# A hybrid gMLP / RG-LRU / HGRN2 layer on one core: empty steps in the heads, set-ups in pieces, earlier loads, another order of the column groups

## Chip, cores and metric

The kernel runs on one core of one Trainium2 chip. The metric is the device time of one execution in microseconds (us). TensorE (PE in the rows) does the matrix products, VectorE (DVE), ScalarE (ACT) and GpSimd (POOL) the elementwise work, SyncE (SP) issues most of the loads. POOL also issues DMAs: all spills, the loads that read a spill back, and the loads that add to what is in place. Each engine works through its own queue in order.

## What is computed

One layer for two groups of rows, 512 prompt rows and 32 sample rows, which share all weights (T = 544 rows, D = 2048):

```python
mod = silu(c) @ w_ada + b_ada
h = rmsnorm(x, norm_g) * (1 + scale) + shift
z = h @ w_in                      # 2048 x 15360
au, av, ag, lx, lg, hq, hf, hi, hg, mg = split(z)
ya = gmlp_mix(gelu(au), rmsnorm(gelu(av)), ws, bs) * silu(ag)
yb = rglru(causal_conv(lx)) * silu(lg)
yc = rmsnorm(hgrn2(silu(hq), hf, hi)) * silu(hg)      # 8 heads, chunks of 64 rows
out = (sigmoid(ga) * (ya @ wb0) + sigmoid(gb) * (yb @ wb1) + sigmoid(gc) * (yc @ wb2)) @ w_out
y = rmsnorm(x + gate * out, final_g)
```

The new states of the three branches are outputs as well.

## The kernel before

Everything is transposed: channels lie on partitions, the 544 rows in the free dimension. Each weight block is split into a high part `wh` (ScalarE, L190) and a low part `wl` (VectorE, L232), and each product is made of three matmuls (`rows3`, L324): wh by the high part of x, wh by its low part, wl by the high part. The product z = h @ w_in (stage z) is made in 60 groups, each of two column blocks of 128; `Group` (from L337) forms the two blocks by seven products of half size in place of eight. So a group has seven **items**, each with 24 large matmuls (128x128 by 128x272), and stage z has 420 items. The second product of a pair needs sums of weight halves: one half is loaded by SP (ring `raw`, five slots, or ring `q`, two slots), the other is added to it in place by a DMA that POOL issues (L266).

The main loop (from L1404) goes over the items. For item i it issues loads (`feed`), then the additions that are due (`load_adds`), then splits the weights of items up to i + 2 (`AHEAD`), then the products of item i and their eviction, and at last calls `pump()`. `load_some` looks nine items ahead, `load_q` six, and both stop where the ring has no free slot; the addition to a q block is put five items ahead of its use.

`pump()` advances every background generator by one step, to its next `yield`: these are the small jobs that use the columns as they come. One step per item is thus their clock. The generators are `av_gen` and `gm_gen` (gMLP), `hg_gen` (one HGRN2 head at a time, 29 items each), `lru_gen` (RG-LRU), `put_away` (a gate, then the spill of a block to DRAM, L1134) and `y_gen` (loads a branch's result, L1199, and splits it for the merges). They share an arena of 32 units in SBUF: a buffer that one has freed is soon taken by another, which then waits until the DMA that spills it has read it.

A head (`hg_gen`) loads `hf` and `hq` (L739), and after two steps makes the gates. Its chunk products go by levels: `lev_d` (POOL, L789) makes differences, `lev_e` exponents (ScalarE), `lev_w` multiplies by k and q (VectorE, L804), `lev_mm` makes the products on TensorE (L815, L817), and `lev_put` (L826) puts them into place. Later come `ew` (VectorE, L882), a one-column product (L885), the load of `hi` (L888), transposes and products (L900 to L972), the load of S0 (L937, on SP), `newton` (L226), the scaling of o (L988) and the transposes of the result (L1003). `hg_setup` (L708) and `lru_setup` (L1017) compute constants once, the first in head 0's first step, the second in the first RG-LRU `post`.

The order of the groups is written out in `z_groups`: four av groups, then sixteen times a head's group (hf with hq, or hi with hg) and a light one (mg, the merge gates, which are only spilled), four light ones, then the 16 heavy ones (gMLP, RG-LRU) with a light one behind every four. A head can start when the spill of its hg is issued.

## Time and profile before

| | us |
|---|---|
| median of 3 runs | 2205.09 (2199.73 to 2208.75) |
| profiled execution, its own time | 2206.34 |
| its span, first to last instruction | 2204.6 |
| mean granted clock of TensorE | 0.956 |

The page of the profile gives for each engine its busy time and its share of the span. A granted clock of 1.00 is TensorE's 2.4 GHz, 0.50 its lower level of 1.2 GHz. From about 133 us to 1671 us stage z runs: the av groups until 244, the heads until 1207, gMLP until 1408, RG-LRU until 1671. Then come the three merges and the output product. In a row of waits the engine that waited stands first, with the line of its waiting instruction, then what ended the wait.

### The profile page before, as it was taken

How to read it: one execution, taken by the hardware profiler on the slowest of the kernel's cores; microseconds unless marked ns; L12 is line 12 of the kernel's file. 1: busy time of each engine (PE TensorE's matmuls, PEld its weight loads, DVE VectorE, ACT ScalarE, POOL GpSimd, SP SyncE). 2: the span in 40 equal slices, each digit the busy share in tenths (PEclk: the TensorE clock that was granted, in tenths of full speed). 3: DMA queues.
4: the chain of work that ended last, by engine and by line, in shares of the span. 5: the costliest groups of instructions: out<-in, count | busy, mean ns of one | idle time of the engine just before them, and what ended most of it. 6: DMA issues, size and time to landing. Idle time of an engine off the chain costs nothing.

```text
span 2204.6 us, 40701 instructions
## 1 busy us (share of the span) xinstructions
PE 2041.6 (93%) x15864; PEld 1945.3 (88%) x15864; DVE 1282.3 (58%) x2204; ACT 1103.0 (50%) x2137; POOL 503.4 (23%) x720
## 2 busy tenths in 40 slices
PE   5789998989998989898999999999987999999997
PEld 3279988989898989897989999999887999999996
DVE  3365665665766575856575766678675433442226
ACT  3357544655555555554554656567565433332223
POOL 0002122232313141313133222112223222220112
PEclk8789998989999999998999999999999999999998
DMA  8977675756665666665667777666655667665554
GB/s 313 365 190 189 187 187 150 189 158 180 168 187 159 179 165 182 162 190 146 188 161 203 188 198 199 180 156 171 166 147 192 232 185 185 195 196 173 174 173 168
DMA packets 135009, 412.22 MB, mean 187 GB/s; under 512 B 16128, under 2 KB 38432, under 8 KB 134816
## 3 DMA queue, kind: packets, MB, share of 16 engines
q1 hardware_dynamic: 87408, 261.08, 35.3%
q0 software_dynamic: 41424, 138.34, 27.7%
q10 hardware_dynamic: 5984, 10.19, 1.5%
q8 instruction: 125, 2.05, 0.4%
q14 instruction: 68, 0.56, 0.1%
HBM read 363.77 MB, written 45.78 MB: 186 GB/s over the span
## 4 chain that ended last, share of the span: by engine, by line
PE 70%; DMA 8%; DVE 7%; issue 6%; ACT 6%; POOL 2%; DVEq 0%; SPq 0%; ACTq 0%; POOLq 0%
PE pm L324 41%; PE pp L324 21%; DMA q<-in_w_in_dram 3%; ACT arena L190 2%; DVE wl L232 2%; ACT wh L190 2%; PE px L815 1%; DMA d_mg<-arena 1%; PE px L1286 1%; PE px L498 1%; PE px L571 1%; DMA raw<-in_w_ss_dram 1%; DVE x L232 1%; POOL arena L789 1%; DMA arena<-d_hf 1%
## 5 line engine op out<-in xcount | busy, mean ns | idle before, releaser
L324 PE MATMUL pm<-x,wh 128*128 128x272 f32 x6720 | 1316.8, 295 | 49.2 <-ACT arena L190 22.6
L324 PEld LDWEIGHTS pm<-x,wh 128*128 128x128 f32 x6720 | 1088.8, 194 | 58.3 <-ACT arena L190 25.0
L324 PE MATMUL pm<-x,wl 128*128 128x272 f32 x3360 | 987.1, 294 | 2.4 <-DVE wl L232 2.4
L232 DVE TENSOR_TENSOR wl<-raw,wh 128x512 fp32r<-128x512 f32 x652 | 458.1, 729 | 385.0 <-ACT wh L190 381.4
L324 PEld LDWEIGHTS pm<-x,wl 128*128 128x128 f32 x3360 | 649.2, 193 | 4.4 <-DVE wl L232 4.2
L190 ACT ACTIVATE wh<-raw 128x512 fp32r<-128x512 f32 x652 | 391.4, 624 | 334.3 <-PE pm L324 238.3
L324 PE MATMUL pp<-x,wh 128*128 128x272 f32 x2560 | 487.6, 290 | 5.9 <-ACT x L190 2.6
L324 PEld LDWEIGHTS pp<-x,wh 128*128 128x128 f32 x2560 | 402.2, 189 | 20.5 <-issue 13.5
L232 DVE TENSOR_TENSOR wl<-q,wh 128x512 fp32r<-128x512 f32 x360 | 256.1, 737 | 225.9 <-ACT wh L190 224.6
L324 PE MATMUL pp<-x,wl 128*128 128x272 f32 x1280 | 369.4, 289 | 0.0
L190 ACT ACTIVATE wh<-q 128x512 fp32r<-128x512 f32 x360 | 215.5, 624 | 137.7 <-PE pm L324 98.7
L190 ACT ACTIVATE arena<-arena 128x544 f32<-128x544 f32 (+5 forms) x310 | 162.8, 554 | 209.5 <-DVE arena L1339 76.7
L324 PEld LDWEIGHTS pp<-x,wl 128*128 128x128 f32 x1280 | 241.4, 189 | 0.2 <-DVE wl L232 0.2
L190 ACT ACTIVATE arena<-pm 128x272 f32<-128x272 f32 x240 | 93.8, 391 | 182.8 <-PE pm L324 139.8
L266 POOL DMA_DIRECT2D q<-in_w_in_dram x60 | 53.5, 892 | 503.4 <-DMA q<-in_w_in_dram 184.0
L365 DVE TENSOR_TENSOR q<-q,raw 128x1024 f32<-128x1024 f32 x120 | 148.7, 1239 | 4.1
L190 ACT ACT_TABLE_LOAD x59 | 75.7, 1283 | 13.1 <-DVE arena L1063 5.3
L266 POOL DMA_DIRECT2D raw<-in_w_in_dram x60 | 54.1, 902 | 107.7 <-DMA raw<-in_w_in_dram 52.2
L789 POOL TENSOR_TENSOR arena<-arena 128x544 f32<-128x544 f32 (+1 forms) x40 | 52.6, 1327 | 60.1 <-PE px L817 18.3
L815 PE MATMUL px<-arena 128*128 128x128 f32 x160 | 32.4, 333 | 26.9 <-DVE arena L804 17.2
L1242 DVE TENSOR_TENSOR arena<-pp,arena 128x544 f32<-128x544 f32 x48 | 34.7, 723 | 37.0 <-PE pp L324 37.0
L1349 POOL TENSOR_TENSOR tail<-tail,arena 128x544 f32<-128x544 f32 (+1 forms) x15 | 18.6, 1242 | 149.5 <-ACT arena L190 149.5
(265 smaller groups left out, 1425.6 us busy)
## 6 DMA issues: line engine op xcount, KB each, us to landing
raw<-in_w_in_dram SPq DMA_DIRECT2D x240, 512.0 KB, 4.7
q<-in_w_in_dram SPq DMA_DIRECT2D x60, 512.0 KB, 5.0
q<-in_w_in_dram POOLq DMA_DIRECT2D x60, 512.0 KB, 6.3
raw<-in_w_in_dram POOLq DMA_DIRECT2D x60, 512.0 KB, 7.4
raw<-in_w_branch_dram SPq DMA_DIRECT2D x48, 512.0 KB, 4.1
raw<-in_w_ss_dram SPq DMA_DIRECT2D x44, 512.0 KB, 7.0
raw<-in_w_out_dram SPq DMA_DIRECT2D x38, 512.0 KB, 4.6
raw<-in_w_gate_dram SPq DMA_DIRECT2D x32, 512.0 KB, 4.6
```

What stands on the lines that cost most here:

```text
L190: return nc.scalar.activation(out, in_, func, **kw)
L232: tt(lo, src, hi.bitcast(F32), op=OP.subtract)
L266: nc.gpsimd.dma_start(out=raws[n], in_=src, accum_op=OP.add)
L324: mm(p, a, rhs(k, r), start=start and i == 0 and q == 0, stop=stop and i == n - 1 and q == 2, **kw)
L365: tt(raws[n], raws[n], raws[m], op=OP.add)
L498: mm(st["xss"][h][:, :HF], ones, st["sq"][q % 2][:, i, h * HF:(h + 1) * HF], start=q == 0 and i == 0, stop=q == 7 and i == 1)
L571: mm(p[32 * i:32 * i + 2, part * 256:part * 256 + 256], cs[:, 4 * q + i, :], w[:, i * 256:(i + 1) * 256], start=q == 0, stop=q == 3)
L789: ptt(v, fv(src, 0, [[2 * m, nb], [m - 1, 2], [1, m]]), fv(src, m - 1, [[2 * m, nb], [0, 2], [0, m]]), op=OP.subtract)
L815: mm(fv(p, 64 * i, [[128, 2], [1, 64]]), x[:, 256 * i + 128:256 * i + 256], fv(x, 256 * i, [[256 + m, 2], [2 * m, nb], [1, m]]), start=Tru ...
L1242: tt(two(g.ap), halves(p), two(g.ap), op=OP.mult)
L1286: mm(p[32 * i:32 * i + 2, :256], cs[:, 4 * q + i, :], w[:, i * 256:(i + 1) * 256], start=q == 0, stop=q == 3)
L1349: ptt(a[:, n], a[:, n], b.ap[:, n], op=OP.add)
```

## The change

It adds one `yield` in `hg_gen` between `lev_w` and `lev_mm` for levels 16 and 8, for 4 and 2, and for 1, and one behind `newton`; a head takes 32 items. `hg_setup` and `lru_setup` become generators of their own with a `yield` between their parts; they start with head 0's first group and with the last light group ahead of the heavy ones. The loads of hf and hq are a function of their own, which the head before calls near its end. `hi` is loaded one step earlier, S0 by POOL instead of SP. Every `put_away` starts with a `yield`. `load_q` looks ten items ahead. The order of the groups has both groups of head 0 first, then a light group in front of each head's group, eight light ones ahead of the heavy ones, and one behind every eight of these. gMLP's `gm_gen` starts with the group's item 6 instead of its item 1. `y_gen` waits three steps between load and use, but for the second half of y0, and splits the first half in twos.

```diff
@@ -716,21 +716,26 @@
         nc.gpsimd.memset(hg["A"].ap, 0.0)
         t = hbuf(len(LEVELS) * 256)
         nc.gpsimd.dma_start(out=t.ap, in_=consts[:, 130:130 + len(LEVELS) * 256])
+        for _ in range(3):
+            yield
         nc.vector.tensor_copy(masks.rearrange("p a e n -> p (a e n)"), t.ap)
         t.free()
+        yield
         d, lb, l1, ln1 = (lbt[:, i, :] for i in range(4))
         x = P("lb", 0, 8)
         tt(d, x, x, op=OP.subtract)
+        yield
         act(d, d, AF.Exp)
+        yield
         nc.vector.reciprocal(lb, d)
         tt(lb, lb, d, op=OP.mult)
         tt(lb, lb, lb, op=OP.subtract)
         ts(l1, lb, -1.0, 1.0, op0=OP.mult, op1=OP.add)
+        yield
         act(ln1, l1, AF.Ln)
-
-    def hg_gen(h):
-        if h == 0:
-            hg_setup()
+        hg["ready"] = True
+
+    def hg_load(h):
         zf = hbuf()
         kq = [hbuf(T), hbuf(T + 1)]
         kb, qb = sorted(kq, key=lambda b: b.col)
@@ -738,8 +743,18 @@
         for b, n in ((zf.ap, "hf"), (qb.ap[:, 1:], "hq")):
             nc.gpsimd.dma_start(out=b, in_=scratch[f"{n} {h}"])
         nc.gpsimd.memset(qb.ap[:, 0:1], 0.0)
-        yield
-        yield
+        hg["in", h] = zf, kb, qb
+
+    def hg_gen(h):
+        while "ready" not in hg:
+            yield
+        if ("in", h) not in hg:
+            hg_load(h)
+            yield
+            yield
+            yield
+        yield
+        zf, kb, qb = hg.pop(("in", h))
         lb, l1, ln1 = (lbt[:, i, h:h + 1] for i in range(1, 4))
         t1, t2, g = hbuf(), hbuf(), zf
         KO = qb.col - kb.col
@@ -839,6 +854,7 @@
         lev_w(16)
         lev_w(8)
         yield
+        yield
         p1, p2 = lev_mm(16), lev_mm(8)
         lev_d(4)
         lev_d(2)
@@ -850,6 +866,7 @@
         yield
         lev_w(4)
         lev_w(2)
+        yield
         yield
         p1, p2 = lev_mm(4), lev_mm(2)
         xs[1].free()
@@ -881,11 +898,12 @@
         ew = ew_t[:, h % 2]
         tt(ew[:, :4], fv(eq.ap, 64, [[128, 4]]), fv(eq.ap, 128, [[128, 4]]), op=OP.mult)
         nc.vector.tensor_copy(ew[:, 4:5], eq.ap[:, T:T + 1])
+        zi = hbuf()
+        nc.gpsimd.dma_start(out=zi.ap, in_=scratch[f"hi {h}"])
+        yield
         p1 = lev_mm(1)
         mm(p1[:NS, 272:273], ke.ap[:, NP:], qb.ap[:, T:T + 1], start=True, stop=True)
         xs[0].free()
-        zi = hbuf()
-        nc.gpsimd.dma_start(out=zi.ap, in_=scratch[f"hi {h}"])
         yield
         nc.vector.tensor_copy(A[:NS, AS + NS:AS + NS + 1], p1[:NS, 272:273])
         lev_put(1, p1)
@@ -934,7 +952,7 @@
         zi.free()
         ke.free()
         s0 = hbuf(256)
-        nc.sync.dma_start(out=s0.ap[:, :128], in_=S0[:, h, :])
+        nc.gpsimd.dma_start(out=s0.ap[:, :128], in_=S0[:, h, :])
         yield
         act(kt.ap, pk, AF.Copy)
         act(vk.ap[:NS], pq[:NS, :256], AF.Copy)
@@ -984,6 +1002,7 @@
         act(r, r, AF.Exp, scale=-0.5)
         yield
         newton(r, m, t)
+        yield
         osb = hbuf(256)
         tt(ob.ap[:, :NP].rearrange("p (w n) -> p w n", w=4), o[:, :NP].rearrange("p (w n) -> p w n", w=4),
            fv(r, 0, [[1, 4], [0, 128]]), op=OP.mult)
@@ -992,6 +1011,8 @@
         at.free()
         vk.free()
         qe.free()
+        if heads["ready"] > h + 1:
+            hg_load(h + 1)
         yield
         nc.gpsimd.dma_start(out=S_new[0, h], in_=S.ap[:, 384:])
         nc.gpsimd.dma_start(out=S_new[1, h], in_=s0.ap[:, 128:])
@@ -1021,7 +1042,9 @@
         e, u, u2, acc, c8, n8 = (lru_c[:, i, :] for i in range(6))
         ts(e, x, -1.0, None, op0=OP.mult)
         tt(e, e, x, op=OP.min)
+        yield
         act(e, e, AF.Exp)
+        yield
         ts(u2, e, 2.0, None, op0=OP.add)
         nc.vector.reciprocal(acc, u2)
         tt(u, e, acc, op=OP.mult)
@@ -1030,6 +1053,8 @@
         for n in (17, 15, 13, 11, 9, 7, 5, 3, 1):
             tt(acc, acc, u2, op=OP.mult)
             ts(acc, acc, 1.0 / n, None, op0=OP.add)
+            if n % 4 == 3:
+                yield
         tt(acc, acc, u, op=OP.mult)
         ts(e, x, -1.0, 0.0, op0=OP.mult, op1=OP.max)
         stt(acc, acc, 2.0, e, op0=OP.mult, op1=OP.add)
@@ -1044,8 +1069,6 @@
             nc.gpsimd.dma_start(out=w[0].ap, in_=lru_w[b].rearrange("p a n -> p (a n)"))
 
         def post(x, lg):
-            if b == 0:
-                lru_setup()
             start(lru_gen(b, x, lg, w[0]))
         return post, fetch
 
@@ -1121,8 +1144,8 @@
 
         def put_away(n, o, on=None):
 
+            yield
             if n[:2] in ("hq", "hg"):
-                yield
                 t = buf()
                 act(t.ap, o.ap, AF.Sigmoid)
                 yield
@@ -1141,10 +1164,7 @@
             def post(*os):
                 for n, o in zip(names, os):
                     g = put_away(n, o, on if n == names[-1] else None)
-                    if n[:2] in ("hq", "hg"):
-                        start(g)
-                    else:
-                        next(g)
+                    start(g)
             return post
 
         def on_head(h):
@@ -1166,14 +1186,16 @@
             heavy.append((B_AU + g, B_AG + g, post, lambda g=g, cell=cell: start(gm_gen(g, cell))))
         for b in range(8):
             heavy.append((B_LX + b, B_LG + b, *lru_post(b)))
-        todo = av
-        for i in range(16):
-            todo += [head[i], light[i]]
-        todo += light[16:20]
-        rest = iter(light[20:])
+        todo = av + head[:2]
+        todo[4] += ({1: lambda: start(hg_setup())},)
+        for i in range(14):
+            todo += [light[i], head[2 + i]]
+        todo += light[14:22]
+        todo[-1] += ({1: lambda: start(lru_setup())},)
+        rest = iter(light[22:])
         for i, (b1, b2, post, at_start) in enumerate(heavy):
-            todo.append((b1, b2, post, {1: at_start}))
-            if i % 4 == 3:
+            todo.append((b1, b2, post, {6 if i < 8 else 1: at_start}))
+            if i % 8 == 7:
                 todo.append(next(rest))
         todo += rest
         todo[-1] += ({1: lambda: start(y_gen(0, (1, 2), 0)), 2: lambda: start(y_gen(0, (1, 2), 1))},)
@@ -1198,7 +1220,8 @@
                 s = scratch[f"y{br} {k + i}"]
                 nc.gpsimd.dma_start(out=b.ap, in_=s if h is None else s[:, h * HF:(h + 1) * HF])
                 bs_.append(b)
-            yield
+            for _ in range(1 if h else 3):
+                yield
             for i, b in enumerate(bs_):
                 if h is None:
                     split_rows(pair, k + i, b.ap)
@@ -1206,7 +1229,7 @@
                     x = X[pair[h]]
                     split(x[:, k + i, 0, :], x[:, k + i, 1, :], b.ap)
                 b.free()
-                if h is None or i == 3:
+                if h is None or i == 3 or h == 0 and i % 2:
                     yield
 
 
@@ -1403,7 +1426,7 @@
         prepared = 0
         def feed(i):
             load_some(items[min(i + 9, len(items) - 1)][4])
-            load_q(items[min(i + 6, len(items) - 1)][5])
+            load_q(items[min(i + 10, len(items) - 1)][5])
 
         for i, (_, mul, post, pre, _, _) in enumerate(items):
             feed(i)
```

On SP, in the weight stream of the av groups (`raw` and `q` are the two rings; the numbers count buffers), before:

```order
L282 DMA raw_1935<-in_w_in_dram 128x1024
L282 DMA q_1937<-in_w_in_dram 128x1024
L282 DMA raw_2008<-in_w_in_dram 128x1024
L282 DMA raw_2105<-in_w_in_dram 128x1024
L282 DMA raw_2150<-in_w_in_dram 128x1024
```

and now:

```order
L282 DMA raw_1871<-in_w_in_dram 128x1024
L282 DMA q_1915<-in_w_in_dram 128x1024
L282 DMA raw_1941<-in_w_in_dram 128x1024
L282 DMA raw_2014<-in_w_in_dram 128x1024
L282 DMA raw_2117<-in_w_in_dram 128x1024
```

The load of the q block stood behind the raw load raw_1935 and was written at the item after it; now it stands in front of that load (here raw_1941), one item earlier, in every group.

On VectorE, head 1 between `lev_w` of levels 16 and 8 and `lev_put` of their products (masks), before:

```order
L804 TENSOR_TENSOR arena<-arena 128x17x2x16
L804 TENSOR_TENSOR arena<-arena 128x34x2x8
L232 TENSOR_TENSOR wl<-q,wh 128x512 x2
L232 TENSOR_TENSOR wl<-raw,wh 128x512 x2
L826 COPY_PREDICATED arena<-masks,px 128x8x16 x2
```

and now:

```order
L819 TENSOR_TENSOR arena<-arena 128x17x2x16
L819 TENSOR_TENSOR arena<-arena 128x34x2x8
L232 TENSOR_TENSOR wl<-q,wh 128x512 x2
L365 TENSOR_TENSOR q<-q,raw 128x1024
L232 TENSOR_TENSOR wl<-raw,wh 128x512 x2
L390 TENSOR_TENSOR arena<-arena,pm_117 128x272
L232 TENSOR_TENSOR wl<-q,wh 128x512 x2
L841 COPY_PREDICATED arena<-masks,px 128x8x16 x2
```

The splits of three items instead of two stand between the two; TensorE's products of these levels come one item later than they did.

On POOL, from the end of head 0 to the first operations of head 1 (with what each waits for; DMASW are DMAs that POOL issued), before:

```order
L996 DMA out_S_new_dram<-arena 128x128
L997 DMA out_S_new_dram<-arena 128x128 [waits DMASW4_49]
L1134 DMA d_hg_4062<-arena 128x544 [waits DMASW5_49,DVE_49,Activation_49]
L1011 DMA d_y_0_4066<-arena 128x544 [waits DMASW7_49,DMASW6_49,DVE_49]
L739 DMA arena<-d_hf_3360 128x544
L739 DMA arena<-d_hq_3456 128x544 [waits DMASW0_49,PE_49]
L740 MEMSET arena 128x1
L266 DMA raw<-in_w_in_dram 128x1024 [waits DMAHW4_49,DMASW1_49,Activation_49]
L753 TENSOR_TENSOR arena<-arena 128x544 [waits DVE_49,Activation_49]
```

and now:

```order
L744 DMA arena<-d_hf_3135 128x544 [waits DMASW7_49,DMASW2_49]
L744 DMA arena<-d_hq_3183 128x544 [waits DMASW3_49,PE_49]
L745 MEMSET arena 128x1
L266 DMA q<-in_w_in_dram 128x1024 [waits DMAHW0_49,DVE_49]
L1017 DMA out_S_new_dram<-arena 128x128 [waits DMASW5_49,Pool_49]
L1018 DMA out_S_new_dram<-arena 128x128 [waits DMASW6_49]
L1157 DMA d_mg_4032<-arena 128x544 [waits DVE_49]
L1157 DMA d_mg_4034<-arena 128x544 [waits DMASW0_49,Activation_49]
L1032 DMA d_y_0_4038<-arena 128x544 [waits DMASW1_49,DVE_49]
L768 TENSOR_TENSOR arena<-arena 128x544 [waits DVE_49,Activation_49]
```

The two loads of head 1 stood behind the state, a spill and the result of head 0; now they stand in front of them, and the light group's two spills lie between them and the head's first operation.

## Rows read from the trace of the kernel before

**Rows 1.** The page: span; busy us, share of the span and instructions of each engine.
```profile
span 2204.6 us, 40701 instructions
...
PE 2041.6 (93%) x15864; PEld 1945.3 (88%) x15864; DVE 1282.3 (58%) x2204; ACT 1103.0 (50%) x2137; POOL 503.4 (23%) x720
```
**Rows 2.** Stages: length; busy PE, PEld, DVE, ACT, POOL; PEclk; DMA share; GB/s.
```profile
244.00:1207.00 963.00, 898.71 (x6871) 871.24 (x6872) 613.95 (x1047) 514.98 (x1045) 263.56 (x359) 0.96 0.64 174
1207.00:1408.00 201.00, 201.00 (x1592) 199.71 (x1591) 138.82 (x221) 117.42 (x194) 49.53 (x78) 1.00 0.71 190
1408.00:1671.00 263.00, 237.50 (x1747) 232.09 (x1746) 195.78 (x354) 162.24 (x288) 54.29 (x116) 0.95 0.60 165
```
**Rows 3.** The chain of waits in the heads' stage: start us, us, what.
```profile
943.95 6.02 PE pm L324 x48
```
**Rows 4.** TensorE's waits, 244 to 1207 us: releaser; us in total, times, longest.
```profile
PE px L815 <- DVE arena L804: 17.2, 7, 4.7
PE px L885 <- DVE arena L875: 15.2, 6, 3.3
PE px L815 <- ACT wh L190: 9.6, 3, 5.9
PE pm L324 <- ACT arena L190: 7.7, 4, 4.1
PE pm L324 <- ACT wh L190: 5.8, 2, 5.1
PE pm L324 <- DVE arena L381: 3.0, 1, 3.0
PE px L1003 <- DVE arena L988: 1.8, 2, 1.3
...
PE px L909 <- DMA arena<-d_hi: 1.8, 2, 1.4
```
**Rows 5.** Stretches table, behind the gap at 338 us (columns as in group 2).
```profile
345.30:350.70 5.40, 5.40 (x27) 5.38 (x26) 2.15 (x8) 1.96 (x5) 2.07 (x2) 0.53 0.78 165
```
**Rows 6.** The chain of waits, hg_setup.
```profile
304.71 6.23 DMA arena<-in_consts_dram
```
**Rows 7.** The chain of waits, first and last operation of lru_setup on VectorE.
```profile
1438.00 0.09 DVE lru_c L1022
...
1444.02 0.07 DVE lru_c L1037
```
**Rows 8.** TensorE's waits, 1408 to 1671 us.
```profile
PE pm L324 <- ACT arena L190: 14.9, 6, 5.7
PE pm L324 <- DVE arena L381: 6.0, 3, 4.4
PE pm L324 <- ACT wh L190: 4.4, 2, 4.2
```
**Rows 9.** The chain of waits, load of hf for head 5 (counted from 0).
```profile
872.51 6.88 DMA arena<-d_hf
```
**Rows 10.** POOL's waits, 244 to 1207 us: releaser; us in total, times, longest.
```profile
POOL q L266 <- DMA q<-in_w_in_dram: 134.9, 19, 12.2
```
**Rows 11.** TensorE's waits, 1545 to 1562 us.
```profile
PE pm L324 <- ACT arena L190: 5.5, 1, 5.5
```
**Rows 12.** The page: POOL's dearest issue: busy us, mean ns; idle before, releaser.
```profile
L266 POOL DMA_DIRECT2D q<-in_w_in_dram x60 | 53.5, 892 | 503.4 <-DMA q<-in_w_in_dram 184.0
```
**Rows 13.** The chain of waits, load of y0's first half.
```profile
1631.70 6.20 DMA arena<-d_y
```
**Rows 14.** The chain of waits, three spills.
```profile
252.63 8.59 DMA d_hf<-arena
...
762.25 8.03 DMA d_mg<-arena
...
1551.77 5.88 DMA d_y<-arena
```
**Rows 15.** TensorE's waits, 1110 to 1135 us.
```profile
PE px L815 <- DVE arena L804: 4.2, 1, 4.2
```

## Prediction

> **What bounds the kernel now.** I read the page's busy table first [rows 1]: TensorE is busy for 2041.6 of 2204.6 us, the next engine, VectorE, for 58%. TensorE sets the time, so the only things to gain are its idle time and the time in which it runs at its lower clock. The second view is the same table cut by stage [rows 2]. The stage of the heads (244 to 1207 us) has 898.71 us of TensorE work in 963.00 us, so 64.3 us idle, at a mean granted clock of 0.96; the RG-LRU stage (1408 to 1671) has 237.50 in 263.00, 25.5 us idle, at 0.95. The gMLP stage between them has no idle time at all and a clock of 1.00. So nearly all that I expect to move lies in two stages.
>
> The third view gives the pitch. In the chain of waits 48 large products take 6.02 us when nothing is late [rows 3]; an item of the program is 24 of them, so one item is 3.01 us. One more empty step between a producer and its consumer therefore buys 3.01 us.
>
> The fourth view says what ends TensorE's idle times in the heads' stage [rows 4]: the products of the levels (L815) wait for VectorE and ScalarE, 17.2 and 9.6 us; the one-column product (L885) waits 15.2 us for VectorE; the large products wait 7.7, 5.8 and 3.0 us, for evictions, splits and sums that are late; two small ones wait 1.8 us each.
>
> **What the clock adds.** After a gap TensorE runs at half rate for a while: in the 5.40 us behind the gap at 338 us it is busy throughout, at a granted clock of 0.53, which is the lower level of 1.2 GHz nearly all of the time [rows 5]. Over the stage the clock costs 963 x (1 - 0.96) = 38.5 us against 64.3 us idle, so a microsecond of gap costs (64.3 + 38.5) / 64.3 = 1.60 us. In the RG-LRU stage 263 x 0.05 = 13.2 us stand against 25.5, a factor of 1.52. I use these two factors for whatever goes and whatever comes.
>
> The Trainium skill, "TensorE: Matmul & The Clock Gate", Part 1, has a rule that speaks against so large a clock term: the ramp is worth less than 1% of a typical kernel's span, which here would be an estimated 22 us for the whole program. The rows have 51.7 us in two stages, so the measurement decides; by the page's figure the clock's part of the gain below (31 us) would shrink to 31 x 22 / 51.7 = 13 us, and the sum would be 2140 us.
>
> **The change, part by part, in idle time of TensorE.**
>
> *Empty steps before the products and behind newton.* The step between the level's product of VectorE and TensorE's use goes from one item to two; L885 gets the same. The waits of L815 are at most 4.7 us behind VectorE and 5.9 us behind ScalarE, in ten waits; those of L885 at most 3.3 in six [rows 4]. Less 3.01 each, L885's are gone: 15.2. Of L815's the three longest would keep some 6 us, but these three have a cause of their own (below), so I take all 26.8 out here and charge that cause anew. The waits of L1003 and L909, 3.6 us, go with the step behind newton and with the earlier load of `hi`. A head now takes 32 items instead of 29. Its work is the same; what it delays is only y2, which the third merge reads over a hundred items later. If that cover were gone, it would cost 8 x 3 x 3.01 = 72 us.
>
> *Set-ups.* hg_setup issues a load of 6.23 us and lets VectorE wait for it at once [rows 6]; the gap is the longest, 5.1 us, of the row of the large products and `wh` [rows 4]. Now three steps (9.0 us) lie behind the issue: gone. lru_setup holds VectorE from 1438.00 to 1444.02 with some 28 small operations in a row [rows 7], and a gap of 4.4 us follows [rows 8]; now it comes before the gMLP items, in pieces of at most nine (2 us): gone.
>
> *Loads of the head's rows.* A load of `hf` lands 6.88 us after its issue [rows 9], and ScalarE uses it two items (6.0 us) after; now it is four items. That and the waits behind late spills are the remaining 11.4 us of the large products [rows 4] (16.5 less 5.1). I take them out too.
>
> *Second q blocks further ahead.* The window grows from six items to ten, but the ring has two slots, and the order shows the load only one item earlier, in front of one raw load instead of behind it. So the addition on POOL, which today waits 134.9 us for that load [rows 10], has two items of distance instead of one. In the RG-LRU stage one gap of 5.5 us [rows 11] begins with ScalarE waiting for such an addition: gone. In the heads this works through the late spills already counted. The raw load behind it loses its place in SP's queue. It cannot gain by that; if it were always the last to arrive, it would lose an issue each time, 0.9 us by the dearest such row [rows 12], 49 us in 54 groups. Since both wait for splits put at the same item, the raw block's own slot is what it waits for, and I take nothing.
>
> *S0 on POOL instead of SP.* Eight more issues on POOL, at most 892 ns each by the row of its dearest issue [rows 12], so 0 to 7 us of POOL's time, and POOL is busy for 263.56 of 963 us [rows 2]: nothing. S0 is used three items (9.0 us) later, which hides its landing.
>
> *y0 loads.* The first half of y0 is used one item after its loads; they land in 6.20 us [rows 13], and the gap is the 4.2 us of the row of `wh` [rows 8]. With three items (9.0 us) it goes. The second half keeps its one item, and its gap (5.7 us, the longest of its row [rows 8]) stays.
>
> *What is late next: handed-over buffers.* A spill is now one item later for mg, hf and hi, and its buffer is taken again soon. The next writer must wait until the spill has landed: d_mg took 8.03 us from issue, d_hf 8.59 [rows 14]. In the order before, seven places in the heads' stage have the writer at most one item behind the spill. Three of them show no gap; the other four show 4.7, 4.1, 5.9 and 4.2 us [rows 4, 15], 2.7 each on average. After the change I count nine such places, two of them ahead of level products, which have an item more: 9 x 2.7 - 2 x 3.0 = 18 us. The bounds are nothing and 9 x 5.9 = 53 us. In the RG-LRU stage five writes of VectorE (L390) now stand one item behind the spill of y1. One such place exists today, with ScalarE writing: the gap of 5.5 us, with POOL late. The spill landed in 5.88 us [rows 14]; less one item 2.9 us are left, about the item by which VectorE works ahead. I take 1.0 each, 5 us, with bounds of 0 and 27.
>
> **The sum.** Heads: 26.8 + 15.2 + 3.6 + 5.1 + 11.4 = 62.1 out, 18 in, net 44, times 1.60 = 70 us. RG-LRU: 4.4 + 4.2 + 5.5 = 14.1 out, 5 in, net 9.1, times 1.52 = 14 us. The profiled execution took 2206.3 us, 1.3 above the median of the runs shown and inside their spread, so I leave that as it is: 2206.3 - 84 = **2122 us**.
>
> **The rivals.**
> - *All gaps close.* The hand-overs cost nothing, as in three of seven places today. 62.1 x 1.60 + 14.1 x 1.52 = 120: 2086 us. For it speaks that the gMLP stage, with the same weight stream, has no gap [rows 2].
> - *The clock does not come back.* The gaps get shorter, but enough stay to pull the clock down as often. Only idle time is won, 44 + 9 = 53: 2153 us. For it: the gaps that I leave standing, at the handed-over buffers, are the long ones, and it is a long gap that the half rate follows [rows 5]. The page of the Trainium skill named above, with its small ramp, points the same way; its 2140 us lie between this and the forecast.
> - *The q load is not really earlier.* SP's queue is in order and waits for the same split, so the extra item is lost. The 5.5 us and one late spill of 4.1 us stay: 9.6 us, 15 with the clock: 2137 us. For it: one item is all that the order shows.
> - *Hand-overs dear.* Each costs 4.1 us in the heads and 3 in the RG-LRU stage: (62.1 - 36.9) x 1.60 + (14.1 - 15) x 1.52 = 39: 2167 us.
> - *Slower.* The same mechanism further out: POOL issues the spills in order behind the additions, and the next writer sits on VectorE or ScalarE, with every split of the weights queued behind it. At p us for each of the fourteen places the price is (9 x 1.60 + 5 x 1.52) p = 22 p; it decides from p = 5.5 on. If the whole landing of 8.03 us stood open, 177 us would come for the 120 that go: 2263 us. Against it: the dearest place today is 5.9, and three cost nothing.
>
> **How the numbers follow.** A measurement of this kernel can tell about 0.5% (11 us) from no change. Forecast (2122) 0.46; all gaps close (2086) 0.13; clock (2153) 0.09; q load (2137) 0.09; dear hand-overs (2167) 0.09; p between 5.0 and 6.0, no change, 0.06; slower 0.08. So faster 0.86, same 0.06, slower 0.08. The range of 2080 to 2182 us takes in the first five cases and leaves out no change, slower and what lies beyond the closing of all gaps.
>
> **What would show it.** Right: the level products' and L885's rows among TensorE's waits shrink to a few us; no gap near the two set-ups; the heads' stage some 70 us shorter at a clock of 0.98 or more; POOL's wait for q loads well under 134.9 us. Wrong: waits of ScalarE or VectorE for a spill (d_mg, d_y) at the head of the list with gaps of over 5 us behind them, a low clock in spite of fewer gaps, or splits waiting for raw loads.

## The result, and the profile after

The changed kernel took 2117.77 us in the median of four runs (2115.85 to 2119.62), the kernel before 2202.41 (2195.36 to 2208.75) beside it: a ratio of 0.9616, 95% interval 0.9583 to 0.9650. The forecast was 2122.

The page after, the lines that answer to [rows 1]:

```profile
span 2114.4 us, 40619 instructions
...
PE 2005.6 (95%) x15864; PEld 1912.6 (90%) x15864; DVE 1288.1 (61%) x2204; ACT 1104.0 (52%) x2137; POOL 519.4 (25%) x728
```

To find the 90 us of span, both traces are cut at the same items of stage z: from the start of item 35, which lies behind the four av groups and the first group of head 0, to that of item 304 (the heads and the first heavy items), to item 360 (gMLP), to the end of stage z (RG-LRU), to the end. Columns as in [rows 2]. Before:

```profile
243.90:1262.60 1018.70, 954.41 (x7311) 926.46 (x7311) 653.79 (x1110) 548.61 (x1099) 279.54 (x385) 0.96 0.64 175
1262.60:1439.50 176.90, 176.49 (x1396) 175.24 (x1396) 119.73 (x195) 98.50 (x168) 38.45 (x59) 1.00 0.72 194
1439.50:1671.50 232.00, 206.89 (x1506) 201.69 (x1504) 175.62 (x316) 148.13 (x263) 49.39 (x109) 0.94 0.58 158
1671.50:2204.60 533.10, 512.11 (x4136) 491.60 (x4136) 213.01 (x379) 182.59 (x339) 115.97 (x133) 0.99 0.61 188
```

After:

```profile
243.40:1195.90 952.50, 923.37 (x7291) 899.50 (x7291) 652.08 (x1115) 538.66 (x1089) 276.18 (x368) 0.99 0.68 186
1195.90:1374.70 178.80, 178.80 (x1415) 177.67 (x1415) 130.59 (x207) 107.27 (x174) 56.90 (x85) 1.00 0.69 194
1374.70:1587.80 213.10, 202.30 (x1506) 196.82 (x1504) 170.51 (x291) 146.73 (x260) 50.78 (x109) 0.98 0.64 175
1587.80:2114.40 526.60, 510.16 (x4137) 489.93 (x4136) 213.02 (x379) 182.30 (x340) 114.55 (x131) 0.99 0.61 190
```

The heads give 66.2 us (forecast 70), RG-LRU 18.9 (forecast 14), gMLP takes 1.9, the merges and the output product give 6.5 that the forecast did not have. In the heads 64.3 us of idle time became 29.1, and the busy time, which is longer where the clock is low, fell by 31.0. Of these 31.0 us 2.9 are twenty small products of `gm_gen` (x7311 became x7291), which now starts later and has them in gMLP's stretch: the clock gives back 28.1, and gMLP's 1.9 are this work.

TensorE's waits in the heads' stage (241 to 1191 us), to be read against [rows 4]:

```profile
PE pm L324 <- ACT arena L190: 15.1, 7, 4.9
PE px L951 <- ACT arena L190: 5.4, 1, 5.4
PE pm L324 <- DVE arena L381: 3.7, 2, 2.5
PE pm L324 <- DVE wl L232: 2.6, 4, 1.3
PE pm L324 <- ACT wh L190: 2.5, 2, 1.5
...
```

The level products (L815, now L830) and the one-column product (L885, now L905) are gone from the list. What is left begins with ScalarE, and its two long gaps have one cause each. The timeline of ScalarE and POOL at them (start, length; in brackets the idle time before and what ended it):

```profile
465.73 0.87 POOL L266 DMA_DIRECT2D q<-in_w_in_dram  x1 [10.75 <-DVE wl L232]
466.28 0.91 POOL L1157 DMA_DIRECT2D d_hi<-arena  x1
...
474.47 1.28 ACT L190 ACT_TABLE_LOAD   x1 [6.64 <-DMA d_hi<-arena]
...
749.39 0.87 POOL L266 DMA_DIRECT2D q<-in_w_in_dram  x1 [3.38 <-DMA q<-in_w_in_dram]
749.95 1.40 POOL L1157 DMA_DIRECT2D d_mg<-arena  x2
...
758.28 1.20 ACT L190 ACTIVATE arena<-arena 128x544 f32<-128x544 f32 x2 [6.68 <-DMA d_mg<-arena]
```

These are handed-over buffers: POOL issues the spill of `hi` or mg behind an addition that it has been waiting for, and ScalarE, which has been given the buffer, stands for 6.6 us until the spill has landed. TensorE's gaps there are 5.4 and 4.9 us.

### The profile page after: what moved, and what is told of

Read it like the earlier page. It is cut to its first block, busy times and chain, and to the rows that moved or that the text cites. A ratio compares the mean times of both kernels' runs of the same rounds, so it can differ in the third digit from the quotient of the medians.

```text
span 2114.4 us, 40619 instructions
## 1 busy us (share of the span) xinstructions
PE 2005.6 (95%) x15864; PEld 1912.6 (90%) x15864; DVE 1288.1 (61%) x2204; ACT 1104.0 (52%) x2137; POOL 519.4 (25%) x728
## 5 line engine op out<-in xcount | busy, mean ns | idle before, releaser
L324 PE MATMUL pm<-x,wh 128*128 128x272 f32 x6720 | 1294.7, 292 | 40.2 <-ACT arena L190 25.0
L324 PEld LDWEIGHTS pm<-x,wh 128*128 128x128 f32 x6720 | 1069.3, 191 | 49.4 <-ACT arena L190 32.2
L324 PE MATMUL pm<-x,wl 128*128 128x272 f32 x3360 | 977.0, 291 | 3.1 <-DVE wl L232 3.0
L232 DVE TENSOR_TENSOR wl<-raw,wh 128x512 fp32r<-128x512 f32 x652 | 467.4, 744 | 361.2 <-ACT wh L190 358.2
L324 PEld LDWEIGHTS pm<-x,wl 128*128 128x128 f32 x3360 | 638.3, 190 | 5.4 <-DVE wl L232 5.4
L1372 POOL TENSOR_TENSOR tail<-tail,arena 128x544 f32<-128x544 f32 (+1 forms) x15 | 18.6, 1239 | 150.7 <-ACT arena L190 150.7
L190 ACT ACTIVATE arena<-px 128x128 f32<-128x128 f32 (+4 forms) x136 | 43.4, 332 | 10.5 <-PE px L1309 4.0
```

The source lines that it names most:

```text
L190: return nc.scalar.activation(out, in_, func, **kw)
L232: tt(lo, src, hi.bitcast(F32), op=OP.subtract)
L324: mm(p, a, rhs(k, r), start=start and i == 0 and q == 0, stop=stop and i == n - 1 and q == 2, **kw)
L1372: ptt(a[:, n], a[:, n], b.ap[:, n], op=OP.add)
```

## The experiments

Four things were open: what the empty steps are worth by themselves, whether the set-ups and the q window do anything, what the handed-over buffers cost before and after, and where the 6.5 us of the merges come from. All ratios are to the kernel before on the same chip; the changed kernel's is 0.9616 (0.9583 to 0.9650). In the first four experiments, all on one chip, the kernel before took 2198.78 us in the median, in the next four, on another, 2205.67, in the last four, on a third, 2201.66. So across these sets the ratios are compared, and a point of the ratio is 22 us. The stages below are cut at the same items as above.

### Without the four empty steps

```diff
@@ hg_gen, in front of the products of levels 16/8, 4/2 and 1, and behind newton
-        yield
```

> The changed kernel without the four empty steps of the heads (before the products of levels 16 and 8, of 4 and 2, of 1, and behind newton); all else stays. Theory A, the steps carry the heads' gain: the waits of the level products, of the one-column product and of the transposes come back, 26.8 + 15.2 + 1.8 = 44 us of idle time, at 1.60 some 70 us, less what the other parts of the change still save there: 2165 to 2190 us, with the level products and the one-column product at the head of TensorE's waits in the heads' stage. Rival B, the other order of the groups and the earlier loads carry it and the steps are a cushion that is hardly used: 2118 to 2133 us, with less than 8 us of waits of the level products.

Measured: 2139.36 us (2138.73 to 2141.07), 0.9727 (0.9703 to 0.9751), some 24 us over the changed kernel by the ratios, between the two theories. TensorE's waits in the heads' stage (the one-column product stands here at L902):

```profile
PE px L902 <- DVE arena L890: 18.1, 8, 3.1
PE pm L324 <- DVE arena L381: 10.5, 8, 2.5
PE px L830 <- DVE arena L819: 9.9, 7, 2.9
...
```

The steps are used at every head: the one-column product's wait is back in full (15.2 before). But the level products wait 9.9 us and not 26.8, at most 2.9 at a time. And the two 5 us gaps above are not there. Handed-over buffers are not gone: ScalarE waits 18.1 us for the DMAs that read the new state, 13.6 for spills of mg and 3.1 for one of hf, yet TensorE waits for ScalarE only twice in this stage, 1.4 us at most. So this run undoes more than the steps, and the question is put again below.

### The q window at six items

```diff
-            load_q(items[min(i + 10, len(items) - 1)][5])
+            load_q(items[min(i + 6, len(items) - 1)][5])
```

> The changed kernel with the window of the q loads at six items again. Theory A, the prediction's term (late additions held up 5.5 us in the RG-LRU stage and one late spill of 4.1 us in the heads): 2117.8 + 5.5 x 1.52 + 4.1 x 1.60 = 2133 us, and POOL's wait for q loads in the heads' stage above today's 104.3 us. Rival B, the load waits for the ring's slot and not for the window, so that one item earlier in SP's order is no earlier landing: within 4 us of 2118, and POOL's wait for q loads as long as now.

Measured: 2111.99 us (2109.42 to 2113.73), 0.9603 (0.9582 to 0.9624), by the ratio 3 us under the changed kernel and not told apart from it: rival B. The larger window gives nothing. The traces show why. In the heads' stage POOL's additions to q wait for the load and for the split that frees its slot. The rows are, in this order, of the kernel before (beside the 134.9 us of [rows 10]), of the changed kernel and of this run:

```profile
POOL q L266 <- DVE wl L232: 33.9, 4, 11.5
...
POOL q L266 <- DMA q<-in_w_in_dram: 104.3, 16, 11.9
POOL q L266 <- DVE wl L232: 95.5, 12, 12.1
...
POOL q L266 <- DVE wl L232: 111.3, 14, 12.7
POOL q L266 <- DMA q<-in_w_in_dram: 91.7, 13, 11.5
```

The wait for the load fell only as the wait for the split grew, and it is shorter still with the old window. With the spills one item earlier (below) it is 151.7 us, and 31.9 for the split. So the shorter wait, which the prediction named as a sign of being right, came with the later spills and not with the window.

### Both set-ups in one piece

```diff
@@ hg_gen
-        while "ready" not in hg:
-            yield
+        if h == 0:
+            for _ in hg_setup():
+                pass
@@ post of the RG-LRU blocks
+            if b == 0:
+                for _ in lru_setup():
+                    pass
@@ z_groups
-        todo[4] += ({1: lambda: start(hg_setup())},)
...
-        todo[-1] += ({1: lambda: start(lru_setup())},)
```

> The changed kernel with both set-ups in one piece at their old places (head 0's first step; the first RG-LRU block). Theory A: both gaps come back, 5.1 x 1.60 + 4.4 x 1.52 = 15 us: 2133 us, with a gap of some 5 us at head 0's start and one of some 4 us at the start of the RG-LRU stage. Rival B: the earlier loads and the longer distances now cover them: 2118 to 2121 us.

Measured: 2118.22 us (2116.71 to 2120.24), 0.9633 (0.9612 to 0.9654). Neither theory fits as a whole: the time stood still, as rival B has it, yet both gaps are back, as theory A has it, of 5.0 us at 286 us and 4.1 at 1395 (TensorE's waits around them):

```profile
PE pm L324 <- ACT wh L190: 5.0, 1, 5.0
...
PE pm L324 <- DVE arena L381: 4.1, 1, 4.1
```

What paid for them are gaps elsewhere that the changed kernel has and this one has not, the one at 472 us among them. An edit anywhere in stage z changes who gets which buffer, and that noise is as large as the terms to be measured.

### The buffer that was freed longest ago

```diff
@@ Arena.find, buffers of two units (free() notes the order in which units were freed)
-            n = self.units // 2
-            for j in range(n):
-                i = 2 * ((self.at + j) % n)
-                if not (b[i] or b[i + 1]):
-                    self.at = (i // 2 + 1) % n
-                    return i
-            return None
+            free = [i for i in range(0, self.units - 1, 2) if not (b[i] or b[i + 1])]
+            return min(free, key=lambda i: max(self.freed[i:i + 2]), default=None)
```

> The changed kernel with another rule for the arena's buffers: of the free pairs of units the one that was freed longest ago is taken, not the next one from a moving mark. Places with at most one item between the issue of a spill and the next writer of its buffer go from 11 to 2 in the heads and from 5 to 0 in the RG-LRU stage. Theory A, handed-over buffers are what is left of the gaps in the heads (the two of about 5 us, at 472 and 757 us, and some of 1 to 3): 12 to 20 us less, 2098 to 2106 us, and ScalarE's waits for spills of d_mg and d_hi (13.7 us) gone. Rival B, these waits only move to another engine or place: 2114 to 2121 us. Rival C, the spills are late because POOL is late, so that the wait stays as long in another form: no less than 2112 us.

Measured: 2086.35 us (2085.24 to 2088.34), 0.9488 (0.9468 to 0.9508), 28 us less than the changed kernel and more than theory A's 20, from a rule that chooses buffers. Not one instruction of work was added or moved in the program. Its stages (heads, RG-LRU, merges and output):

```profile
243.00:1175.70 932.70, 916.78 (x7291) 893.81 (x7291) 655.05 (x1115) 539.81 (x1089) 276.62 (x368) 1.00 0.68 189
...
1354.50:1557.10 202.60, 197.62 (x1506) 194.10 (x1504) 169.98 (x291) 146.57 (x261) 54.49 (x109) 0.99 0.65 182
1557.10:2083.50 526.40, 510.16 (x4137) 489.95 (x4136) 212.77 (x379) 182.22 (x339) 113.72 (x131) 0.99 0.60 190
```

The heads lose 19.8 us, RG-LRU 10.5. ScalarE no longer waits for a spill of d_mg or d_hi in the heads' stage. No later run is told apart from this one as faster, and it is the quiet base on which the next runs test the parts again.

### The kernel before with that rule

```diff
@@ Arena.find, in the kernel before; nothing else
-            n = self.units // 2
...
+            return min(free, key=lambda i: (-runs(i), max(self.freed[i:i + 2])), default=None)
```

(`runs` counts the runs of three free units that the choice would leave, up to two.)

> The kernel before with nothing changed but the arena's rule: of the free pairs of units the one freed longest ago is taken (where that leaves room for two buffers of three units). Places with a writer at most one item behind the spill of its buffer go from eight to four in the heads and from one to none in the RG-LRU stage. Theory A, handed-over buffers made the longest gaps of the kernel before too: 4.7, 4.1, 5.9, 4.2 and 5.5 us of idle time go, less some 2.5 us at each of three that stand before level products, which keep their short distance: 17 us, at 1.5 to 1.6 some 26 us, a ratio to the kernel before of 0.984 to 0.991. Rival B, the waits are the splits' and the additions' and find another place: 0.995 to 1.005.

Measured: 2169.76 us (2168.11 to 2173.35), 0.9838 (0.9822 to 0.9853): theory A, at the far edge of its range and 10 us more than the 26 it named. The rule takes 36 us out of the kernel before. Heads and RG-LRU:

```profile
242.10:1236.30 994.20, 939.47 (x7311) 913.13 (x7311) 666.04 (x1110) 548.44 (x1099) 284.17 (x385) 0.98 0.66 179
...
1412.50:1631.20 218.70, 203.40 (x1506) 199.02 (x1504) 174.86 (x316) 147.93 (x263) 49.26 (x109) 0.96 0.62 167
```

24.5 us came out of the heads, 13.3 out of RG-LRU. The gap of 5.5 us [rows 11] that the prediction gave to a late q addition is gone here although the q window is the old one. In the kernel before ScalarE writes there, one item behind it, into the buffer that the spill of d_y1 reads, and waits 7.7 us for that; POOL is late with this spill because it waits 6.5 us for VectorE, not for an addition.

What the buffers did not take is as telling. In the heads the level products still wait 21.3 us (here L824 behind L813), against 26.8 in [rows 4]:

```profile
PE px L824 <- DVE arena L813: 18.6, 9, 3.6
...
PE px L824 <- ACT wh L199: 2.7, 2, 1.7
```

### The empty steps on the quiet base

```diff
@@ hg_gen, with the rule of the longest free buffer
-        yield
```

> The changed kernel with the rule of the longest free buffer and without the four empty steps of the heads. Theory A, the steps have a value of their own, apart from the hand-overs: 18.1 + 9.9 + 3.8 = 32 us of waits as in the run without steps, which with the clock make 32 to 50 us on 2086: 2118 to 2136 us. Rival B, steps and a better hand-over do the same work twice: at most 15 us, 2101 us or less.

Measured: 2123.93 us (2120.84 to 2128.88), 0.9630 (0.9611 to 0.9648): 1.42 points over 0.9488, 31 us, the low end of theory A (32 to 50). The heads' stage and its waits (the level products stand here at L828, the one-column product at L900):

```profile
244.30:1211.20 966.90, 926.38 (x7291) 900.46 (x7291) 651.63 (x1116) 540.37 (x1089) 280.99 (x372) 0.99 0.67 183
```

```profile
PE px L900 <- DVE arena L888: 17.6, 8, 2.7
...
PE px L828 <- DVE arena L817: 8.2, 7, 1.5
PE px L1018 <- DVE arena L1001: 3.9, 7, 0.6
```

The stage is 34.2 us longer (966.9 to 932.7). Four empty steps, which do nothing, are worth 31 to 34 us.

### The set-ups on the quiet base

```diff
@@ hg_gen and post, with the rule of the longest free buffer; edit as above
-        while "ready" not in hg:
-            yield
+        if h == 0:
+            for _ in hg_setup():
+                pass
...
```

> The changed kernel with the rule of the longest free buffer and both set-ups in one piece at their old places. In the run with the set-ups alone undone both gaps came back (5.0 and 4.1 us), and yet the time stood still, with other gaps at handed-over buffers gone. Theory A, that was a coincidence of the buffers: with hand-overs out of the way the set-ups cost what the prediction gave them, 12 to 15 us on 2086: 2098 to 2101 us. Rival B, they cost nothing: 2083 to 2090 us.

Measured: 2099.01 us (2095.81 to 2100.40), 0.9513 (0.9498 to 0.9527). The medians are 12.7 us apart, the ratios, from two sets of runs of the kernel before, 5.5. The stages of the profiled runs tell more:

```profile
243.90:1178.70 934.80, 916.16 (x7293) 892.61 (x7291) 653.00 (x1093) 539.53 (x1091) 280.32 (x370) 1.00 0.69 190
...
1357.50:1570.60 213.10, 201.82 (x1506) 198.00 (x1504) 174.73 (x321) 149.06 (x264) 54.43 (x109) 0.97 0.64 172
```

Heads 2.1 us longer, RG-LRU 10.5, together 12.6: theory A by the traces of one execution each, while the intervals of the two ratios overlap. The split is not clean. TensorE's gap at hg_setup is 5.3 us, but the heads' idle time grew by 2.7, so other waits there fell; in RG-LRU it grew by 6.3, of which 4.1 are the gap at lru_setup and the rest longer waits near the loads of y0, where ScalarE waits 5.5 us for a spill of y1.

### The second half of y0 like the first

```diff
-            for _ in range(1 if h else 3):
+            for _ in range(3):
...
-                if h is None or i == 3 or h == 0 and i % 2:
+                if h is None or i % 2:
```

> The changed kernel with the rule of the longest free buffer, and the second half of y0 loaded and split like the first (three steps between, splits in twos). Theory A, the slow items at the end of the stage (7 us over the pitch in two items) are this half's: 4 to 7 us less than 2086, 2079 to 2082 us. Rival B, the splits now end later and the first merge starts later by as much: 2083 to 2090 us.

Measured: 2091.96 us (2089.45 to 2092.61), 0.9481 (0.9465 to 0.9496): no difference to 0.9488, rival B. RG-LRU is 1.1 us shorter (201.5), the stretch behind it 4.6 longer (531.0). On this base the gap at the second half is only 1.1 us, so there was little left to gain.

### The buffer that was freed last

```diff
@@ Arena.find, the opposite rule
-            return min(free, key=lambda i: max(self.freed[i:i + 2]), default=None)
+            return max(free, key=lambda i: max(self.freed[i:i + 2]), default=None)
```

> The changed kernel with the opposite rule: of the free pairs of units the one that was freed last is taken. Places with a writer at most one item behind the issue of the spill go from 11 to 24 in the heads (twelve of them in the same item) and from 5 to 6 in the RG-LRU stage. It tests how far the prediction's slower rival reaches. Theory A, the wait is the rest of the landing time: some 5.5 us at each of the twelve in the same item, 2.7 at the others, 12 x 5.5 + 12 x 2.7 = 98 us of idle time, and 6 us in the RG-LRU stage, at 1.5 some 156 us over the 2086 of the run with the oldest buffer: 2210 to 2250 us, slower than the kernel before. Rival B, a place costs what the step from 16 places to two gave on the mean, 2.0 us with the clock: 30 places, 2086 + 60 = 2146 us, still faster than before.

Measured: 2279.31 us (2272.54 to 2285.16), 1.0357 (1.0323 to 1.0390). With the same work in the same order the change is now slower than the kernel before, by more than theory A gave. Its stages, and ScalarE's waits in the heads:

```profile
244.60:1292.20 1047.60, 951.59 (x7291) 921.63 (x7291) 646.34 (x1115) 535.57 (x1089) 277.38 (x368) 0.96 0.61 169
...
1471.00:1713.60 242.60, 209.56 (x1506) 201.01 (x1504) 170.35 (x291) 147.65 (x260) 56.77 (x109) 0.96 0.56 153
1713.60:2276.80 563.20, 521.63 (x4137) 496.78 (x4136) 204.94 (x379) 178.31 (x340) 110.23 (x131) 0.98 0.57 177
```

```profile
ACT L188 <- DMA d_hf<-arena: 52.2, 7, 10.8
ACT L188 <- DMA d_hi<-arena: 50.1, 7, 10.0
```

Seven of the eight heads pay twice: some 7 us at the spill of hf and as much at that of `hi`. The heads are 114.9 us longer than with the oldest buffer, RG-LRU 40.0. The merges are 36.8 us longer, which the expectation, that stopped at stage z, had not.

### The loads of y as before

```diff
@@ y_gen, with the rule of the longest free buffer
-            for _ in range(1 if h else 3):
-                yield
+            yield
...
-                if h is None or i == 3 or h == 0 and i % 2:
+                if h is None or i == 3:
```

> The changed kernel with the rule of the longest free buffer, and the loads of the branches' results as they were (one step between load and use, first half of y0 in fours). Theory A: the gap of 4.2 us at the first half of y0 comes back, 4.2 x 1.52 = 6 us, and the merges begin as late as in the kernel before, where the stretch behind the last item of stage z was 6.5 us longer, which the prediction did not have: 2086 + 13 = 2099 us. Rival B, the 6.5 us come from elsewhere (the clock, the spills): 2092 us. Rival C, nothing: 2086 us.

Measured: 2103.80 us (2101.64 to 2105.84), 0.9560 (0.9533 to 0.9586), 16 us over 0.9488: theory A in sum (13), not in its parts. RG-LRU takes 11.1 us more (213.7 to 202.6), the stretch behind it 3.8 (530.2 to 526.4):

```profile
1358.20:1571.90 213.70, 202.12 (x1506) 198.05 (x1504) 171.01 (x292) 147.26 (x261) 51.69 (x109) 0.97 0.63 174
1571.90:2102.10 530.20, 511.83 (x4137) 491.51 (x4136) 214.12 (x378) 183.04 (x339) 113.41 (x131) 0.99 0.60 188
```

### The spills one item earlier

```diff
@@ put_away and its start, in the changed kernel with its own rule
-            yield
             if n[:2] in ("hq", "hg"):
+                yield
...
-                    start(g)
+                    if n[:2] in ("hq", "hg"):
+                        start(g)
+                    else:
+                        next(g)
```

> The changed kernel with the spills one item earlier again, as before (mg, hf and hi spilled in the item that makes them). Handed-over places fall from 11 to seven in the heads, five in the RG-LRU stage stay. Theory A, the prediction's: the later spill only makes hand-overs tighter, so undoing it gives four places back, some 2 us each with the clock: 2106 to 2112 us. Rival B, the later spill keeps POOL's queue from waiting for an eviction ahead of the additions, so undoing it costs: 2122 us or more. Rival C, where the buffers fall decides and not their number: 2112 to 2122 us.

Measured: 2123.12 us (2119.11 to 2123.93), 0.9643 (0.9616 to 0.9670): not told apart from the changed kernel, though four handed-over places fewer stand in it. Theory A falls. Rival B does not: 2123 lies in its range too, and in the heads POOL waits 21.6 us to spill mg behind its eviction. One of the seven left alone costs a gap of 6.7 us at 437 us, where POOL itself was given the buffer that it had just spilled:

```profile
430.93 0.88 POOL L1157 DMA_DIRECT2D d_hf<-arena  x1
439.07 2.23 POOL L804 TENSOR_TENSOR arena<-arena 128x544 f32<-128x544 f32 x2 [7.26 <-DMA d_hf<-arena]
```

The level differences that POOL makes there are needed by ScalarE, and behind ScalarE wait the splits. This place shows that where a hand-over stands counts, and not only how many there are, as rival C has it; how the time divides between B and C is open.

### The q window on the quiet base

```diff
@@ feed, with the rule of the longest free buffer
-            load_q(items[min(i + 10, len(items) - 1)][5])
+            load_q(items[min(i + 6, len(items) - 1)][5])
```

> The changed kernel with the rule of the longest free buffer and the window of the q loads at six items. The run with the window alone undone was 3 us faster, at other hand-overs' gaps. Theory A, the prediction's term is real and was covered by them: 2086 + 8 to 15 = 2094 to 2101 us. Rival B, the ring's two slots set the load, the window does nothing: 2083 to 2090 us.

Measured: 2086.94 us (2083.42 to 2088.12), 0.9481 (0.9454 to 0.9508): rival B again, the window is worth nothing.

Not tried: the empty steps alone in the old order, the old order of the groups alone, and the heads without the early loads of their rows. Each keeps more buffers in use at once than the arena's 32 units hold, so these parts cannot be had one by one.

## Why the prediction was right, and where it was not

The time, its stages and the main cause hold: TensorE's idle time in two stages, and behind it the clock. That the sum came within 5 us is in part luck. The steps stood in it some 40 us too high and the q blocks 8. What made up for it: the loads of y stood 9 too low, the order of the groups had no term, and the hand-overs of the kernel before, at which the rule of the longest free buffer takes out 36 us, were spread over other terms. With that rule on both sides the change gives 3.5 points (0.9838 to 0.9488), 77 us. Its steps one by one:

- **Empty steps.** "L885's are gone", and L815's: right, the rows have left the list. The size is not: 26.8 + 15.2 + 3.6 = 45.6 us of idle time, 73 with the clock, stood in the sum; the run on the quiet base shows 31 to 34 in time. The mis-sized term is the 26.8 of L815, of which only 8 to 10 us belong to the short distance in the new order. The prediction charged the long waits among them anew to buffers; but with the rule of the longest free buffer the kernel before still has 21.3 of them (18.6 and 2.7), so buffers took some 5. The other 11 to 13 went with other parts of the change, since the changed kernel without the steps has 8.2 to 9.9; the order of the groups and the early loads are the likeliest, and which of them it was is open.
- **Set-ups.** 8 + 7 us forecast. The gaps are as they were read (5.3 and 4.1 us when put back), and undoing both makes the two stages 12.6 us longer, 2.1 in the heads and 10.5 in RG-LRU. The sum is near; what each set-up is worth is not shown, as other waits moved too.
- **Loads of the head's rows.** 11.4 us of idle time were taken out. Not tested alone. With the rule of the longest free buffer on both sides, the heads are 994.2 us before and 932.7 after; 34.2 of these 61.5 are the steps, 2.1 the set-up, and the other 25 are left for the order of the groups, the early loads and what hand-overs each of the two still has, together.
- **Second q blocks.** "In the RG-LRU stage one gap of 5.5 us begins with ScalarE waiting for such an addition: gone." This step failed: two runs give the window nothing, and the gap went in the kernel before by the buffers' rule alone. The rival that the load is not really earlier was right on the mechanism and wrong on the time, since the gap did not hang on the load.
- **y0.** 4.2 x 1.52 = 6 us forecast, 11.1 measured in the stage and 3.8 in the merges, which were not in the sum; the other 2.7 of the merges' 6.5 are open. That the second half keeps its gap was right; the changed kernel has 5.6 us there, where ScalarE waits 3.9 us for these loads. With the oldest buffer the gap shrank to 1.1 us and that wait is gone; why the loads are in time there is open.
- **Handed-over buffers.** 18 us in the heads and 5 in RG-LRU, with the clock 36; the rule of the longest free buffer takes out 28 (19.8 and 10.5 of span). The size was near. The count was not: what was expected of the later runs goes by eight places in the heads before and 11 after, and not seven and nine. Nor were the places in RG-LRU: VectorE waits 12.8 us at the five writes at L390, but none shows a gap of TensorE of more than 0.6 us.
- **The clock.** A factor of 1.60 for whatever goes. Between the two traces the heads lost 35.2 us of idle time and, without the moved products, 63.3 in all, 1.80 times as much, so the rival in which the clock does not come back falls. The Trainium skill, "TensorE: Matmul & The Clock Gate", Part 1, puts the penalty of the ramp at under 1% of a typical kernel's span, an estimate of 22 us at most for this program. The 28.1 us that came back in this stage alone are more, and the measurement decides.
- **The slower rival.** It put the turn at 5.5 us per hand-over and the end at 2263 us. The run with the newest buffer ended at 2279 by this mechanism, so such an end was within reach; that it did not happen was the luck of which buffers were free. The price was not right: the 30 places counted in the heads and RG-LRU made these stages 154.9 us longer than with the oldest buffer, some 5 us each with the clock, where the rival had 177 us for fourteen places, 12.6 each; the merges, which it did not have, gave the other 36.8. The 0.08 rested on a count of places, and the count did not tell the cost.
- **S0 on POOL, and three items more in a head.** Taken at nothing and not tested alone. POOL's busy time in the whole program rose from 503.4 to 519.4 us, of which S0's eight issues are 5.1; no engine's wait names S0's load. ScalarE's waits for loads of the branches' results fell from 20.0 to 3.9 us, and none is left in the merges, so the later y2 cost nothing there.

The change as it stands is worth 3.8%; with the rule of the longest free buffer added it is 5.1% (0.9488, 2086 us). The rule by itself gives the kernel before 1.6%.

## What to carry to other kernels

Where buffers come from a shared pool, look at which is given out: take the one freed longest ago before tuning anything else, since a spill in flight here holds its buffer for 3.3 to 7.0 us more in the median and the engine that gets it stands with all its queue. Measure edits of the schedule on that base; otherwise each one reshuffles the buffers, and the shuffle can hide a gain of 12 us, as it did for the set-ups. An empty step between producer and consumer is cheap where something else fills the engine, but size it by the waits that are left when buffers do not disturb, not by the row as it stands.

## What had not been expected of the hardware

What the clock costs does not follow the length of the gaps. In the run with the newest buffer TensorE waits 8.5 us from 446.5 us on. Here are the stretch behind this gap in which it is busy throughout, at the lower level of 1.2 GHz, and the one behind the gap of 4.7 us in the kernel before, from its first product on:

```profile
455.00:460.60 5.60, 5.60 (x24) 5.60 (x25) 5.57 (x9) 2.41 (x5) 0.59 (x1) 0.50 0.41 143
...
342.60:350.20 7.60, 7.59 (x33) 7.08 (x34) 4.51 (x11) 1.96 (x5) 3.16 (x3) 0.50 0.69 170
```

Behind the longer gap the low clock lasted 5.6 us, behind the shorter one 7.6; [rows 5] shows only the later part of these 7.6. In these runs long gaps carry the smaller surcharge: that run has 96.0 us of idle time in the heads' stage and the kernel before 64.3, both at a mean clock of 0.96. And short ones may carry next to none: without the steps on the quiet base 40.5 us are idle (966.90 less 926.38), most of it in waits of under 3 us, at 0.99. By these three runs one factor for all gaps, as in the prediction, is too coarse.

The second is how long a spill holds its buffer. By the table of DMA issues of the changed kernel, with KB of each and the median us from issue to landing,

```profile
q<-in_w_in_dram POOLq DMA_DIRECT2D x60, 512.0 KB, 7.1
...
d_mg<-arena POOLq DMA_DIRECT2D x48, 272.0 KB, 6.8
...
d_y<-arena POOLq DMA_DIRECT2D x24, 272.0 KB, 3.3
d_hf<-arena POOLq DMA_DIRECT2D x8, 272.0 KB, 7.0
```

the same 272 KB take 7.0 us for hf and 3.3 for y. The Trainium skill, "DMA: Bandwidth & Descriptors", Anatomy of one DMA, has a fixed 2.0 us and 436 GB/s for a DMA on GpSimd's path, an estimate of 2.6 us for this size. Beside the weight stream and its additions only y comes near it, so the measured values stand. What stands in front of a spill goes with the difference: of the 104 spills of these kinds in this trace, 63 are issued while an addition of POOL's to a weight block is still in flight. All 63 land behind that addition, after 7.0 us in the median; the other 41 take 3.7. In the kernel before it is 60 at 6.3 us and 44 at 4.4. Whether a spill issued ahead of the addition would free its buffer sooner, no run tested.
